# Eight-chunk operand tiles, a bonus by split products, and later joins in a hybrid decoder block

## The chip, the cores and the metric

The kernel runs on one core of one Trainium2 chip. The core has TensorE (PE), whose matrix products write to PSUM, VectorE (DVE), ScalarE (ACT), GpSimd (POOL) and SyncE (SP, which here only issues transfers); each works through its own instructions in order. The metric is the device time in microseconds of one execution, lower is better.

## The reference, cut to what matters

One decoder block on 2048 tokens of width 1024, in float32. The first stage is the one that the change concerns. Half of the mixer is RWKV-7 time mixing with 8 heads of 64:

```python
h = rmsnorm(x, norm_mix[l])
p = h @ w_in[l]
y_ret = retention_mixer(p[..., :RET_PROJ], ...)      # chunks of 128
y_rwkv = rwkv7_mixer(p[..., RET_PROJ:], ...)
...
def step(state, inp):                                # in wkv7_scan, one token after the other
    r_t, w_t, k_t, v_t, a_t, b_t = inp
    sa = jnp.einsum('bhvk,bhk->bhv', state, a_t)
    state = (state * w_t[:, :, None, :] + sa[..., None] * b_t[:, :, None, :]
             + v_t[..., None] * k_t[:, :, None, :])
    return state, jnp.einsum('bhvk,bhk->bhv', state, r_t)
...
bonus = jnp.sum(rh * kh * r_k.astype(jnp.float32), axis=-1, keepdims=True) * vh
return (y + bonus.reshape(B, S, W)) * g
```

Then `x + y @ w_out`, a cross-attention into 256 memory tokens, an MLP with a squared ReLU and a last RMS norm.

## The kernel before, in words

The work has two stages. The first makes the mixer's output and the products of the memory's weights; the second, of two halves of 1024 tokens, does the rest. The change lies in the first.

There the recurrence is computed in chunks of 64 tokens. A **block** is 512 tokens (8 chunks) of one pair of heads, so there are 16 blocks, numbered by `n = 4 * b + pr`; in tile names the two digits are `b` and `pr` (block 5 is `11`, block 8 is `20`). A pair's two heads lie on the two halves of the partitions (`hs[0]`, `hs[1]`). For each block:

- `rwkv_prep` makes the operands: from keys, decays and rates the tiles `BK` and `kk`, then `AR` (the scaled keys and receptances of each chunk, later overwritten in its other half by masked products `psc`), `SR`, `X` (whose other half receives the values, through the products `pvt` and a ScalarE copy, L516) and `BKt` (the transposition `pk` of `BK`). It ends with the bonus: `rS` becomes r times k times r_k, an fp32 product with a matrix of ones sums it over each head (`pb`), and the result is multiplied into the values.
- `diagonal` inverts the 16x16 diagonal pieces of the chunk matrices by small VectorE steps (`Tm`, `Tb`), and `inverses` joins them to inverses of 64x64: VectorE transposes (`TD`, L579), TensorE multiplies (`ph_1`, `ph_2`), VectorE transposes again (`TA`, L593), and TensorE multiplies (`pg_1`, `pg_2`). These four products are called the join below.
- `rwkv_chain` runs the chunks one after the other, each with three hops on TensorE (`ch`) and writes by VectorE, ScalarE and GpSimd between them (`rh`, `X`, `Sd`); the state travels through `X`.

The dense products (`mm..`, `rmq`, `rmv`: projections of the input, in three split products hi x hi, hi x lo, lo x hi each, of operands in fp32r) stand between all of this. The order of TensorE's instructions is fixed by `weave`: eight streams (chains, diagonals, joins, preparations, retention heads, post-processing, transpositions of the input, dense work) are generators. A stream's `yield u` says that its next step is written only after `u` us of TensorE work by the writer's own estimates (`te["us"]`), and meanwhile the other streams, in the order of the list, write theirs. TensorE executes exactly in that order. VectorE's, ScalarE's and GpSimd's orders are set by the framework's scheduler, after priorities and a time line of its own. PSUM has two banks for the small products of this stage (`ps_sc`, tag `sc`), used in turn, so that the second transposition `pk_1` writes the bank out of which `X` is copied.

`split(hi, lo, x, eng)` writes x as a sum of two fp32r tiles: a ScalarE copy (L183) and a subtraction on VectorE or GpSimd (L184).

Of the kernel before, what the change touches and what calls it, by code (L numbers as in the profile page):

```python
# [125 lines left out]
def hybrid_block(tc, a, out, dbg=None, halves=2, stages="012"):  # L126
# [154 lines left out]
    if "1" in stages:  # L281
        with ExitStack() as ctx:
# [65 lines left out]
            def rotary_tables():  # L348
# [18 lines left out]
                AQ.dma_start(out=rot[:, :, 0, :], in_=t3(cc))  # L367
                AQ.dma_start(out=rot[:, :, 1, :], in_=t3(nn))


            Sst = one.tile([P, 4, C], F32, name="Sst")
            V.memset(Sst, 0.0)
# [25 lines left out]
            def rwkv_prep(n, pr, tok0, kS, wa, nm):  # L398
# [82 lines left out]
                AR, SR, X, BKt = ([], []), [], ([], []), []  # L481
                yield lambda: ("R", n) in done and ("C", n - 2, NCH) in done
                rS, vS = done["R", n]
                for g in range(2):
                    for h in range(2):
                        ar = gp.tile([P, 4, P], F32, tag=f"AR{h}", name=f"AR{h}{nm}_{g}", bufs=4)
                        AR[h].append(ar)
                        A.activation(out=ar[hs[h], :, 0:C], in_=ch(kk)[hs[h], g4[g]], func=AF.Copy, scale=-1.0)
                        V.tensor_tensor(out=ar[hs[h], :, C:], in0=ch(rS)[hs[h], g4[g]], in1=Pe[hs[h], g4[g], 1:], op=ALU.mult)
                yield LAT[7]  # L490
                for g in range(2):
                    sr = gp.tile([P, 4, C], F32, tag="SR", name=f"SR{nm}_{g}", bufs=4)
                    SR.append(sr)
                    psc = [ps_sc.tile([P, 4, P], F32, tag="sc", name=f"psc{nm}_{g}{h}") for h in range(2)]
                    for i in range(4):
                        for h in range(2):
                            mm(psc[h][:, i, :], BK[hs[h], 4 * g + i, :, :], AR[h][g][hs[h], i, :], True, True)
                    bc = lambda rows, c0, c1: mk[rows, :, c0:c1].broadcast_to([64, 4, c1 - c0])
                    for h in range(2):
                        q = hs[1 - h]  # L500
                        V.tensor_tensor(out=AR[h][g][q], in0=psc[h][q], in1=bc(q, 0, P), op=ALU.mult)
# [51 lines left out]
            def inverses(n, Mx, TT, nm):  # L553

                a_, b_ = [slice(0, 32), slice(64, 96)], [slice(32, 64), slice(96, 128)]
                TA = gp.tile([P, NCH, 32], F32, tag="TA", name=f"TA{nm}", bufs=1)

                def step(j, rows, op, dst):
                    pg = ps_sc.tile([P, NCH, 32], F32, tag="sc", name=f"pg{nm}_{j}")
                    for c in range(NCH):  # L560
                        for h in range(2):
                            op(pg[rows[h], c, :], c, h)
                    for h in range(2):
                        A.activation(out=dst(h), in_=pg[rows[h]], func=AF.Copy)


                q_ = [slice(32 * q, 32 * q + 32) for q in range(4)]
                own = lambda q: 32 * (q % 2)
                TD = gp.tile([P, NCH, C], F32, tag="TD", name=f"TD{nm}", bufs=1)
                TC = gp.tile([P, NCH, 16], F32, tag="TC", name=f"TC{nm}", bufs=1)  # L570

                def half(j, op, rows=32):
                    pg = ps_sc.tile([P, NCH, 16], F32, tag="sc", name=f"ph{nm}_{j}")
                    for c in range(NCH):
                        for q in range(4):
                            op(pg[32 * q : 32 * q + rows, c, :], c, q)
                    return pg

                tc.keep_in_program_order(V.transpose(TD.rearrange("p c t -> p (c t)"), TT.rearrange("p c t -> p (c t)")))  # L579
                yield 1.5  # L580
                pg = half(1, lambda o, c, q: mm(o, Mx[q_[q], c, own(q) : own(q) + 32], TD[q_[q], c, own(q) : own(q) + 16], True, True))
                A.activation(out=TC, in_=pg, func=AF.Copy)
                yield LAT[6]
                pg = half(2, lambda o, c, q: mm(o, TC[q_[q], c, :], TT[q_[q], c, own(q) + 16 : own(q) + 32], True, True), 16)
                for q in range(4):
                    src = pg[32 * q : 32 * q + 16]
                    dst = TT[32 * q : 32 * q + 16, :, own(q) + 16 : own(q) + 32]
                    if q % 2:
                        V.tensor_copy(out=dst, in_=src)
                    else:  # L590
                        A.activation(out=dst, in_=src, func=AF.Copy)
                for h in range(2):
                    V.transpose(TA[a_[h]], TT[a_[h], :, 0:32])  # L593
                yield 2.0
                step(1, b_, lambda o, c, h: mm(o, Mx[a_[h], c, 32:64], TA[a_[h], c, :], True, True), lambda h: TA[b_[h]])
                yield LAT[6]
                step(2, a_, lambda o, c, h: mm(o, TA[b_[h], c, :], TT[b_[h], c, 32:64], True, True), lambda h: TT[a_[h], :, 32:64])
                done["pg", n] = True

            def rwkv_chain(n, pr, tok0, nm, SR, AR, X, BKt, TT, PC, rn, bon):  # L600

                Y = ps_y.tile([P, NCH, C], F32, tag="y", name=f"Y{nm}")
                for h in range(2):
                    G.tensor_copy(out=X[h][0][hs[h], 0, :], in_=Sst[hs[h], pr, :])
                for c in range(NCH):
                    g, i = divmod(c, 4)
                    chp = ps_ch.tile([P, 512], F32, tag="ch", name=f"ch{nm}_{c}")
                    Sd = gp.tile([P, C], F32, tag="Sd", name=f"Sd{nm}_{c}")
                    rh = gp.tile([P, C], F32, tag="rh", name=f"rh{nm}_{c}")
                    for h in range(2):  # L610
                        mm(chp[hs[h], 0:64], AR[h][g][:, i, 0:C], X[h][g][:, i, :], True, True)
                    with tc.high_priority(URGENT):
                        V.tensor_copy(out=rh, in_=chp[:, 0:64])
                        for h in range(2):
                            G.tensor_scalar(out=Sd[hs[h], :], in0=X[h][g][hs[h], i, :], scalar1=PC[hs[h], c : c + 1],  # L615
                                            scalar2=None, op0=ALU.mult)
                    yield HOP[0]
                    for h in range(2):
                        mm(chp[hs[h], 64:128], TT[hs[h], c, :], rh[hs[h], :], True, True)
                    for h in range(2):  # L620
                        mm(Y[hs[h], c, :], X[h][g][:, i, :], AR[h][g][:, i, C:], True, False)
                    with tc.high_priority(URGENT):
                        A.activation(out=X[0][g][hs[0], i, :], in_=chp[hs[0], 64:128], func=AF.Copy, scale=rn[hs[0], c : c + 1])  # L623
                        V.tensor_scalar(out=X[1][g][hs[1], i, :], in0=chp[hs[1], 64:128], scalar1=rn[hs[1], c : c + 1],
                                        scalar2=None, op0=ALU.mult)
                    yield HOP[1]
                    for h in range(2):
                        mm(chp[hs[h], 128:192], BKt[g][:, i, hs[h]], X[h][g][:, i, :], True, True)
                    for h in range(2):
                        mm(Y[hs[h], c, :], X[h][g][hs[h], i, :], SR[g][hs[h], i, :], False, True)  # L630
                    with tc.high_priority(URGENT):
                        for h in range(2):
                            dst = X[h][(c + 1) // 4][hs[h], (c + 1) % 4, :] if c + 1 < NCH else Sst[hs[h], pr, :]
# [785 lines left out]
```

## Time and profile before

| | |
|---|---|
| median of 3 runs | 3496.29 us (3493.16 to 3503.72) |
| profiled execution | 3505.42 us, span 3503.4 us |
| TensorE products | 3337.0 us busy, 95% of the span, 23328 instructions |
| TensorE weight loads | 2734.7 us, 78% (they overlap the products) |
| VectorE | 2086.9 us, 60%, 3657 instructions |
| ScalarE | 1223.3 us, 35%, 1974 instructions |
| GpSimd | 1619.2 us, 46%, 1325 instructions |
| mean granted TensorE clock | 0.976 |

A share is an average over two stages with different neighbours of TensorE. Matrix products are pipelined, so a row's length is more than the time until the next can start; that time is the distance between the starts of two rows. An fp32 product shows as two records. The granted clock is 1.0 at 2.4 GHz and 0.5 at 1.2 GHz.

### The profile page before, as it was taken

The numbers are of one execution on the slowest core, as the hardware profiler recorded it, in microseconds if no ns is written. First come the engines' busy times: TensorE is split into PE (matmuls) and PEld (weight loads), VectorE is DVE, ScalarE is ACT, GpSimd is POOL, SyncE is SP. The second block draws the span as 40 slices with busy tenths as digits, with TensorE's granted clock in tenths as the row PEclk, the third lists the DMA queues.
The fourth block names the chain that finished last, engine by engine and source line by source line (L and its number), as shares of the span: only waits on it lengthen the run. The fifth ranks groups of instructions, "written<-read, shape, count | busy, mean of one in ns | idle before, by whom it ended". The sixth has DMA issues, their size and how long they took to land.

```text
span 3503.4 us, 57596 instructions
## 1 busy us (share of the span) xinstructions
PE 3337.0 (95%) x23328; PEld 2734.7 (78%) x23328; DVE 2086.9 (60%) x3657; ACT 1223.3 (35%) x1974; POOL 1619.2 (46%) x1325
## 2 busy tenths in 40 slices
PE   7899999999999999989999999999999999999998
PEld 6667777777787777878887888888788878888886
DVE  5755565456645654544775565566648765556557
ACT  4442333233323232434344333333443343333333
POOL 5544323232323232434456555555645465555555
PEclk9999999999999999999999999999999999999999
DMA  7434333333333332473111111111441111111111
GB/s 254 156 131 157 130 98 112 113 130 99 118 113 119 96 113 98 146 282 103 43 49 43 55 55 49 54 54 50 147 142 49 37 49 55 48 55 55 49 55 48
DMA packets 147160, 333.35 MB, mean 95 GB/s; under 512 B 52048, under 2 KB 62800, under 8 KB 146896
## 3 DMA queue, kind: packets, MB, share of 16 engines
q1 hardware_dynamic: 129632, 299.43, 25.7%
q10 hardware_dynamic: 17264, 30.26, 2.4%
q8 instruction: 183, 3.00, 0.4%
q14 instruction: 81, 0.66, 0.1%
HBM read 269.34 MB, written 60.29 MB: 94 GB/s over the span
## 4 chain that ended last, share of the span: by engine, by line
PE 50%; DVE 5%; issue 2%; ACT 1%; POOL 1%; DVEq 0%; POOLq 0%; ACTq 0%
PE up L141 20%; PE o L141 4%; PE tms L141 4%; PE m3d L141 3%; PE m6d L141 3%; PE m4d L141 2%; PE m2d L141 2%; PE m1d L141 2%; PE m5d L141 2%; PE m7d L141 2%; DVE xr L1146 2%; DVE pe L1258 1%; PE pskv L141 1%; PE m3v L141 1%; PE psqk L141 1%
## 5 line engine op out<-in xcount | busy, mean ns | idle before, releaser
L141 PE MATMUL up<-uc,whi 128*128 128x512 f32 x2048 | 633.2, 390 | 5.6 <-ACT uc L1117 5.6
L141 PEld LDWEIGHTS up<-uc,whi 128*128 128x128 f32 x2048 | 384.4, 188 | 86.8 <-ACT uc L1117 6.6
L141 PE MATMUL up<-uc,wlo 128*128 128x512 f32 x1024 | 398.9, 390 | 0.0
L184 POOL TENSOR_TENSOR wlo<-wraw,whi 128x1024 fp32r<-128x1024 f32 x103 | 253.2, 2459 | 281.3 <-ACT whi L183 268.3
L183 ACT ACTIVATE whi<-wraw 128x1024 fp32r<-128x1024 f32 x175 | 184.7, 1058 | 390.5 <-PE up L141 139.5
L615 POOL TENSOR_SCALAR Sd<-X,PC 64x64 f32<-64x64 f32 x256 | 123.9, 484 | 312.3 <-DVE X L634 298.2
L184 DVE TENSOR_TENSOR wlo<-wraw,whi 128x1024 fp32r<-128x1024 f32 x72 | 104.1, 1446 | 255.8 <-ACT whi L183 255.7
L184 POOL TENSOR_TENSOR wlo<-s,whi 128x1024 fp32r<-128x1024 f32 x60 | 159.4, 2658 | 180.5 <-ACT whi L183 180.5
L141 PEld LDWEIGHTS up<-uc,wlo 128*128 128x128 f32 x1024 | 192.3, 188 | 40.1
L141 PE MATMUL tms<-whi,ub 128*128 128x256 f32 x1024 | 192.2, 286 | 0.0
L184 POOL TENSOR_TENSOR wlo<-bd,whi 128x1024 fp32r<-128x1024 f32 x64 | 166.0, 2595 | 51.5 <-ACT whi L183 51.5
L184 POOL TENSOR_TENSOR f<-au,f 128x1024 fp32r<-128x1024 f32 x40 | 112.2, 2804 | 133.6 <-ACT f L183 133.6
L141 PE MATMUL o<-whi,f 128*128 128x512 f32 x512 | 162.6, 398 | 1.4 <-issue 1.4
L141 PEld LDWEIGHTS tms<-whi,ub 128*128 128x128 f32 x1024 | 161.1, 191 | 0.4
L141 PE MATMUL rmq<-whi,hh 128*128 128x256 f32 x512 | 150.5, 294 | 0.0
L141 PE MATMUL rmq<-whi,hl 128*128 128x256 f32 x512 | 149.8, 293 | 0.0
L141 PE MATMUL rmq<-wlo,hh 128*128 128x256 f32 x512 | 149.8, 292 | 0.0
L141 PE MATMUL tms<-wlo,ub 128*128 128x256 f32 x512 | 145.4, 284 | 0.0
L1305 ACT ACTIVATE au<-up 128x512 f32<-128x512 f32 x128 | 75.2, 587 | 194.6 <-PE up L141 194.6
L623 ACT ACTIVATE X<-ch,rn 64x64 f32<-64x64 f32 x128 | 39.3, 307 | 282.5 <-PE Y L141 266.7
L1077 POOL TENSOR_TENSOR s<-bd,bd 128x1024 f32<-128x1024 f32 x48 | 122.2, 2548 | 33.8 <-DMA bd<-w_down 29.4
L183 ACT ACTIVATE whi<-bd 128x1024 fp32r<-128x1024 f32 x64 | 67.6, 1057 | 189.3 <-PE m2d L141 63.6
(1065 smaller groups left out, 9181.5 us busy)
## 6 DMA issues: line engine op xcount, KB each, us to landing
bd<-w_down SPq DMA_DIRECT2D x64, 512.0 KB
wraw<-w_up SPq DMA_DIRECT2D x64, 512.0 KB
whi<-kepthiw SPq DMA_DIRECT2D x45, 512.0 KB
wlo<-keptlow SPq DMA_DIRECT2D x45, 512.0 KB
whi<-kepthim SPq DMA_DIRECT2D x36, 512.0 KB
wlo<-keptlom SPq DMA_DIRECT2D x36, 512.0 KB
wraw<-w_out SPq DMA_DIRECT2D x32, 512.0 KB
xs<-x SPq DMA_DIRECT2D x16, 512.0 KB
```

The costliest lines, as they stand in the source:

```text
L141: pinned(TE.matmul(o, l, r, start=start, stop=stop), us)
L183: A.activation(out=hi, in_=x, func=AF.Copy)
L184: eng.tensor_tensor(out=lo, in0=x, in1=hi.bitcast(F32), op=ALU.subtract)
L615: G.tensor_scalar(out=Sd[hs[h], :], in0=X[h][g][hs[h], i, :], scalar1=PC[hs[h], c : c + 1], scalar2=None, op0=ALU.mult)
L623: A.activation(out=X[0][g][hs[0], i, :], in_=chp[hs[0], 64:128], func=AF.Copy, scale=rn[hs[0], c : c + 1])
L1077: eng.tensor_tensor(out=into, in0=x, in1=y, op=op)
L1146: V.tensor_tensor(out=xv, in0=xv, in1=ps, op=op)
L1258: V.tensor_scalar(out=pe[:, t, :], in0=pe[:, t, :], scalar1=sm[:, t : t + 1], scalar2=None, op0=ALU.mult)
L1305: A.activation(out=r, in_=ps, func=AF.Relu)
```

## The change

`AR` and `X` become one tile of eight chunks for each head instead of two of four (two buffers instead of four, so the same memory), and each is written by one instruction instead of two. The copies into `X` now stand right behind the products `pvt`, and the second head's goes to VectorE. The bonus's `rS` is split in two fp32r tiles, which are multiplied with an fp32r copy of the ones (made once). In `inverses` two yields are doubled.

```diff
+            ones_r = one.tile([P, P], F32R, name="ones_r")
+            A.activation(out=ones_r, in_=c_("ones"), func=AF.Copy)
...
-                for g in range(2):
-                    for h in range(2):
-                        ar = gp.tile([P, 4, P], F32, tag=f"AR{h}", name=f"AR{h}{nm}_{g}", bufs=4)
-                        AR[h].append(ar)
-                        A.activation(out=ar[hs[h], :, 0:C], in_=ch(kk)[hs[h], g4[g]], func=AF.Copy, scale=-1.0)
-                        V.tensor_tensor(out=ar[hs[h], :, C:], in0=ch(rS)[hs[h], g4[g]], in1=Pe[hs[h], g4[g], 1:], op=ALU.mult)
+                for h in range(2):
+                    ar = gp.tile([P, NCH, P], F32, tag=f"AR{h}", name=f"AR{h}{nm}", bufs=2)
+                    AR.append(ar)
+                    A.activation(out=ar[hs[h], :, 0:C], in_=ch(kk)[hs[h]], func=AF.Copy, scale=-1.0)
+                    V.tensor_tensor(out=ar[hs[h], :, C:], in0=ch(rS)[hs[h]], in1=Pe[hs[h], :, 1:], op=ALU.mult)
...
+                for h in range(2):
+                    x = gp.tile([P, NCH, C], F32, tag=f"X{h}", name=f"X{h}{nm}", bufs=2)
+                    if h:
+                        V.tensor_copy(out=x[hs[1 - h]], in_=pv_[hs[1 - h]])
+                    else:
+                        A.activation(out=x[hs[1 - h]], in_=pv_[hs[1 - h]], func=AF.Copy)
+                    X.append(x)
                 yield 0
...
-                    for h in range(2):
-                        x = gp.tile([P, 4, C], F32, tag=f"X{h}", name=f"X{h}{nm}_{g}", bufs=4)
-                        A.activation(out=x[hs[1 - h]], in_=pv_[hs[1 - h], g4[g], :], func=AF.Copy)
-                        X[h].append(x)
                     yield 0.8
...
-                mm(pb, c_("ones"), rS, True, True)
+                rh_ = tp.tile([P, BLK], F32R, tag="E", name=f"rh{nm}b")
+                rl_ = tp.tile([P, BLK], F32R, tag="A", name=f"rl{nm}b")
+                split(rh_, rl_, rS, V)
+                mm(pb, ones_r, rh_, True, False)
+                mm(pb, ones_r, rl_, False, True)
...
-                yield 1.5
+                yield 3.0
                 pg = half(1, lambda o, c, q: mm(o, Mx[q_[q], c, own(q) : own(q) + 32], TD[q_[q], c, own(q) : own(q) + 16], True, True))
...
-                yield 2.0
+                yield 4.0
                 step(1, b_, lambda o, c, h: mm(o, Mx[a_[h], c, 32:64], TA[a_[h], c, :], True, True), lambda h: TA[b_[h]])
```

The remaining lines of the diff only follow the tiles' new indices (`X[h][:, c, :]` for `X[h][g][:, i, :]`).

TensorE's order before, in the join of block 5, from its second product to its third (`rsR` are products of a retention head, `pss` and the `mm12` rows belong to the preparation of the next block):

```order
L141 MATMUL ph_2_5729<-TT_162,TC_5635 16x16 x32
L141 MATMUL ch_4_5625<-X_10_1_4788,BKt_1_4801 64x64
...
L141 MATMUL Y_5239<-SR_1_4645,X_10_1_4790 64x64
L141 MATMUL rsR_5774<-qkTR_5676 128x128
...
L141 MATMUL rsR_5775<-qkTR_5725 128x128
L141 MATMUL pg_1_5788<-TA_5633,Mx_4984 32x32 x16
L141 MATMUL ch_5_5807<-X_10_1_4788,AR_10_1_4550 64x64
```

And the same place now:

```order
L141 MATMUL ph_2_5692<-TT_164,TC_5575 16x16 x32
L141 MATMUL ch_4_5601<-X_10_4712,BKt_1_4749 64x64
...
L148 MATMUL pqR_5737<-cs,rq_5504 128x128 x4
L141 MATMUL mm12r<-hl,whi_5560 128x512
L141 MATMUL mm12r<-hh,wlo_5561 128x512
...
L141 MATMUL rsR_5749<-qkTR_5688 128x128
...
L141 MATMUL ch_5_5763<-X_10_4712,AR_10_4503 64x64
L141 MATMUL ch_5_5763<-X_10_4714,AR_10_4506 64x64
L141 MATMUL pss_5771<-cs,sq_5628 64x1 x16
L141 MATMUL pg_1_5791<-TA_5573,Mx_4921 32x32 x16
```

A transposition and five dense products have moved ahead of the third product, and so have the next chunk's first chain product and `pss`, which followed it.

ScalarE's order before, at the copies into `X` of block 8 (`rb` is the last step of the post-processing of an earlier block that ScalarE has there):

```order
L388 ACTIVATE ts21r<-mm21r,pv 128x512
L659 ACTIVATE rb_8721<-st_13_8718 128x512
L516 ACTIVATE X_20_0_8754<-pvt_8732 64x256
L516 ACTIVATE X_20_0_8756<-pvt_8732 64x256
L516 ACTIVATE X_20_1_8769<-pvt_8732 64x256
L516 ACTIVATE X_20_1_8771<-pvt_8732 64x256
L520 ACTIVATE BKt_0_8762<-pk_0_8749 128x512
```

And now, on the same engine:

```order
L391 ACTIVATE ts21r<-mm21r,pv 128x512
L668 ACTIVATE rb_8613<-st_13_8610 128x512
L516 ACTIVATE X_20_8706<-pvt_8689 64x512
L525 ACTIVATE BKt_0_8719<-pk_0_8710 128x512
L525 ACTIVATE BKt_1_8730<-pk_1_8721 128x512
```

One copy of twice the width stands where four stood, behind the same `rb`. The other head's copy is in VectorE's order, between steps of the next block's diagonal inversion:

```order
L550 TENSOR_TENSOR Tb_8491<-Tb_8491,Tm_8615 128x8x9
L546 TENSOR_TENSOR Tm_8615<-Lb_8489,Tb_8491 128x8x8
L514 COPY X_20_8708<-pvt_8689 64x512
L550 TENSOR_TENSOR Tb_8491<-Tb_8491,Tm_8615 128x8x8
L546 TENSOR_TENSOR Tm_8615<-Lb_8489,Tb_8491 128x8x7
```

Before, no row of VectorE stood there for `X`.

## Rows read from the trace of the kernel before

**Rows 1.** Stretches: their length, then busy us (instructions) by engine, clock, DMA.

```profile
0.00:1480.00 1480.00, 1371.74 (x13844) 1096.94 (x13845) 849.53 (x2134) 474.72 (x943) 528.62 (x824) 0.96 0.39 128
1480.00:3503.00 2023.00, 1965.21 (x9486) 1637.73 (x9484) 1237.35 (x1524) 748.53 (x1032) 1090.57 (x502) 0.99 0.21 71
```

**Rows 2.** TensorE's waits, 0 to 1480 us: us in total, times, longest.

```profile
PE pg L141 <- DVE TA L593: 15.9, 9, 4.6
PE pk L148 <- ACT X L516: 13.4, 8, 3.8
PE ch L141 <- DVE X L624: 13.4, 16, 2.8
...
PE ch L141 <- DVE X L634: 5.6, 8, 1.4
...
PE ph L141 <- DVE TD L579: 3.9, 4, 1.3
```

**Rows 3.** TensorE's time line at block 1's bonus: start, us, instruction.

```profile
149.94 0.39 PE L141 MATMUL mm02r<-hh,wlo 128*128 128x512 f32 x1
150.17 1.02 PE L141 MATMUL pb<-rS01r,cs 128*128 128x512 f32 x2
151.12 0.34 PE L141 MATMUL ch<-X,AR 128*64 128x64 f32 x4
```

**Rows 4.** Instructions by tile or line, ns min/median/max; the last row: busy, mean ns.

```profile
L516 ACT ACTIVATE X<-pvt x64: 358/378/382, 95.2 to 1346.5; 64x256 f32<-64x256 f32 x64
L520 ACT ACTIVATE BKt<-pk x32: 577/597/600, 96.6 to 1351.9; 128x512 f32<-128x512 f32 x32
L184 DVE TENSOR_TENSOR wa<-wf,wa 128x512 fp32r<-128x512 f32 x3 | 2.1, 686 | 0.5 <-ACT wa L183 0.5
```

**Rows 5.** Time line at block 8's copies into X.

```profile
787.37 0.63 ACT L659 ACTIVATE rb<-st 128x512 f32<-128x512 f32 x1 [7.07 <-POOL st L681]
...
788.01 1.55 ACT L516 ACTIVATE X<-pvt 64x256 f32<-64x256 f32 x4
...
789.61 0.66 PE L148 MATMUL pk<-cs,BK 128*128 128x128 f32 x4 [3.83 <-ACT X L516]
```

**Rows 6.** Time line of block 5's join; in brackets the idle time before.

```profile
505.22 1.16 PE L141 MATMUL rsR<-qkTR 64*128 64x128 f32 x16
...
509.58 0.60 DVE L634 SCALAR_TENSOR_TENSOR X<-ch,PC,Sd 64x64 f32<-64x64 f32 x2
...
511.01 0.31 PE L141 MATMUL pg<-TA,Mx 32*32 32x32 f32 x2 [4.63 <-DVE TA L593]
...
512.60 0.44 DVE L593 STREAM_TRANSPOSE TA<-TT 32x256 f32<-32x256 f32 x1
513.09 1.06 PE L141 MATMUL pg<-TA,Mx 32*32 32x32 f32 x30 [1.77 <-DVE TA L593]
```

**Rows 7.** TensorE's time line in block 13's join.

```profile
1210.96 0.31 PE L141 MATMUL pg<-TA,Mx 32*32 32x32 f32 x2 [4.63 <-DVE TA L593]
1211.74 1.05 PE L141 MATMUL pg<-TA,Mx 32*32 32x32 f32 x30 [0.47 <-DVE TA L593]
```

**Rows 8.** Five short stretches at clock 0.50, the first and the sum.

```profile
575.72:579.13 3.41, 3.15 (x10) 1.88 (x8) 3.25 (x8) 2.73 (x5) 2.52 (x3) 0.50 0.00 0
...
sum 20.47, PE 20.21 PEld 14.33 DVE 10.90 ACT 7.07 POOL 6.76; mean PE 4.04 PEld 2.87 DVE 2.18 ACT 1.41 POOL 1.35
```

**Rows 9.** Four long stretches at clock 0.50, that of block 5 and the sum.

```profile
507.45:521.11 13.66, 8.33 (x121) 6.96 (x122) 6.00 (x13) 2.60 (x7) 3.80 (x5) 0.50 0.00 1
...
sum 54.61, PE 42.69 PEld 31.54 DVE 21.36 ACT 14.60 POOL 16.42; mean PE 10.67 PEld 7.88 DVE 5.34 ACT 3.65 POOL 4.11
```

**Rows 10.** Time line of VectorE's diagonal steps beside GpSimd.

```profile
93.35 4.68 POOL L184 TENSOR_TENSOR wlo<-wraw,whi 128x1024 fp32r<-128x1024 f32 x2 [6.96 <-ACT whi L183]
...
95.90 2.23 DVE L537 TENSOR_TENSOR Tm<-Lb,Tb 128x72 f32<-128x72 f32 x1
...
98.16 0.23 DVE L541 TENSOR_TENSOR Tb<-Tb,Tm 128x72 f32<-128x72 f32 x1
```

More of the change, by code (lines that the diff above doesn't have):

```diff
@@ L479, in rwkv_prep @@
                 done["L", n] = Lb, Tb, Mx, TT_[gi % 2], Ts, nm
-                AR, SR, X, BKt = ([], []), [], ([], []), []
+                AR, SR, X, BKt = [], [], [], []
                 yield lambda: ("R", n) in done and ("C", n - 2, NCH) in done
                 rS, vS = done["R", n]
-                for g in range(2):
-                    for h in range(2):
-                        ar = gp.tile([P, 4, P], F32, tag=f"AR{h}", name=f"AR{h}{nm}_{g}", bufs=4)
-                        AR[h].append(ar)
-                        A.activation(out=ar[hs[h], :, 0:C], in_=ch(kk)[hs[h], g4[g]], func=AF.Copy, scale=-1.0)
-                        V.tensor_tensor(out=ar[hs[h], :, C:], in0=ch(rS)[hs[h], g4[g]], in1=Pe[hs[h], g4[g], 1:], op=ALU.mult)
+                for h in range(2):
[3 more added lines that the diff above has]
+                    V.tensor_tensor(out=ar[hs[h], :, C:], in0=ch(rS)[hs[h]], in1=Pe[hs[h], :, 1:], op=ALU.mult)
                 yield LAT[7]
@@ L496, in rwkv_prep @@
                         for h in range(2):
-                            mm(psc[h][:, i, :], BK[hs[h], 4 * g + i, :, :], AR[h][g][hs[h], i, :], True, True)
+                            mm(psc[h][:, i, :], BK[hs[h], 4 * g + i, :, :], AR[h][hs[h], 4 * g + i, :], True, True)
                     bc = lambda rows, c0, c1: mk[rows, :, c0:c1].broadcast_to([64, 4, c1 - c0])
@@ L500, in rwkv_prep @@
                         q = hs[1 - h]
-                        V.tensor_tensor(out=AR[h][g][q], in0=psc[h][q], in1=bc(q, 0, P), op=ALU.mult)
+                        V.tensor_tensor(out=AR[h][q, g4[g]], in0=psc[h][q], in1=bc(q, 0, P), op=ALU.mult)
                         V.tensor_tensor(out=sr[hs[h]], in0=psc[h][hs[h], :, C:], in1=bc(hs[h], C, P), op=ALU.mult)
@@ L603, in rwkv_chain @@
                 for h in range(2):
-                    G.tensor_copy(out=X[h][0][hs[h], 0, :], in_=Sst[hs[h], pr, :])
+                    G.tensor_copy(out=X[h][hs[h], 0, :], in_=Sst[hs[h], pr, :])
                 for c in range(NCH):
@@ L610, in rwkv_chain @@
                     for h in range(2):
-                        mm(chp[hs[h], 0:64], AR[h][g][:, i, 0:C], X[h][g][:, i, :], True, True)
+                        mm(chp[hs[h], 0:64], AR[h][:, c, 0:C], X[h][:, c, :], True, True)
                     with tc.high_priority(URGENT):
@@ L614, in rwkv_chain @@
                         for h in range(2):
-                            G.tensor_scalar(out=Sd[hs[h], :], in0=X[h][g][hs[h], i, :], scalar1=PC[hs[h], c : c + 1],
+                            G.tensor_scalar(out=Sd[hs[h], :], in0=X[h][hs[h], c, :], scalar1=PC[hs[h], c : c + 1],
                                             scalar2=None, op0=ALU.mult)
@@ L620, in rwkv_chain @@
                     for h in range(2):
-                        mm(Y[hs[h], c, :], X[h][g][:, i, :], AR[h][g][:, i, C:], True, False)
+                        mm(Y[hs[h], c, :], X[h][:, c, :], AR[h][:, c, C:], True, False)
                     with tc.high_priority(URGENT):
-                        A.activation(out=X[0][g][hs[0], i, :], in_=chp[hs[0], 64:128], func=AF.Copy, scale=rn[hs[0], c : c + 1])
-                        V.tensor_scalar(out=X[1][g][hs[1], i, :], in0=chp[hs[1], 64:128], scalar1=rn[hs[1], c : c + 1],
+                        A.activation(out=X[0][hs[0], c, :], in_=chp[hs[0], 64:128], func=AF.Copy, scale=rn[hs[0], c : c + 1])
+                        V.tensor_scalar(out=X[1][hs[1], c, :], in0=chp[hs[1], 64:128], scalar1=rn[hs[1], c : c + 1],
                                         scalar2=None, op0=ALU.mult)
@@ L627, in rwkv_chain @@
                     for h in range(2):
-                        mm(chp[hs[h], 128:192], BKt[g][:, i, hs[h]], X[h][g][:, i, :], True, True)
+                        mm(chp[hs[h], 128:192], BKt[g][:, i, hs[h]], X[h][:, c, :], True, True)
                     for h in range(2):
-                        mm(Y[hs[h], c, :], X[h][g][hs[h], i, :], SR[g][hs[h], i, :], False, True)
+                        mm(Y[hs[h], c, :], X[h][hs[h], c, :], SR[g][hs[h], i, :], False, True)
                     with tc.high_priority(URGENT):
                         for h in range(2):
-                            dst = X[h][(c + 1) // 4][hs[h], (c + 1) % 4, :] if c + 1 < NCH else Sst[hs[h], pr, :]
+                            dst = X[h][hs[h], c + 1, :] if c + 1 < NCH else Sst[hs[h], pr, :]
                             V.scalar_tensor_tensor(out=dst, in0=chp[hs[h], 128:192], scalar=PC[hs[h], c : c + 1],
```

## The prediction

> **What bounds the kernel now.** I read the page first: TensorE is busy for 95% of the span, VectorE for 60%, so a change shows only where it alters what TensorE does or waits for. Every edit lies in the first stage, up to about 1480 us, and the table by stretches splits the span there [rows 1]: TensorE is idle for 108 us of those 1480 and its mean granted clock is 0.96, against 58 us idle and 0.99 in the other 2023. Those 108 us, and the time that the clock stands at 1.2 GHz, are the most that a better order can win; the work itself is the rest. TensorE's list of waits in that stage names what ends them [rows 2]. The largest entry is the join's first product (pg) behind VectorE's transposition TA, 15.9 us in nine waits. The second is the transposition pk behind ScalarE's copies of X, 13.4 us in eight. The chain's products (ch) behind VectorE's writes of X cost 13.4 + 5.6 us, and the join's earlier product (ph) behind the transposition TD costs 3.9 us with none above 1.3. The change touches all five.
>
> The sums below are waits and work of the profiled execution, which took 3505.4 us (span 3503.4 and 2.0 around it), 9.1 above the median of the runs, 3496.3. I subtract the sum from the median. About 0.3%, 10.5 us, is what a measurement of this kernel can tell from no change.
>
> **The bonus product.** The timeline shows the fp32 product pb starting at 150.17 and the next product at 151.12, so it holds TensorE for 0.95 us [rows 3]. A split (fp32r) product of the same 128x512 shape is the row ahead of it, 149.94 to 150.17, 0.23 us. Two of them take 0.46, so each of the 16 blocks saves 0.49 us: **-7.8 us**, and this is work, not a wait. If the weight load of the second product were not covered it would be less; as the row of 0.23 us is one of a stream with changed weights, I keep the value, with -4 as the poorer bound (half of it). The price is one more ScalarE copy and one more VectorE subtraction of 128x512 in each block, 0.60 us by BKt's copy of that size and 0.69 by the split of wa [rows 4]. By the order both stand many instructions ahead of pb, before the block's products of AR, so TensorE doesn't wait for them: cost nothing while that lead holds, and 16 x 1.29 = 21 us if it were gone. The buffers that they take (of kk and Pi) are free by then, and the next block's first writes of them come behind pb's place in TensorE's order anyway.
>
> **The eight-chunk tiles.** AR's writes become half as many and twice as long. Nothing in rows 2 waits for them, so I give that nothing; a first product that needs the whole tile comes some 0.3 us later than behind a half. For X, four ScalarE copies of 0.378 us (1.51) [rows 4] become one of twice the width, about 0.60 by BKt's row, and one on VectorE, about 0.69 by wa's. pk's second transposition writes the bank that the copies read, so it waits for the last. Block 8 shows it: ScalarE finishes rb, then copies X from 788.01 for 1.55 us, and pk starts at 789.61 after 3.83 us of idle [rows 5]. The order leaves rb ahead of X, so the wait shrinks by 0.91 us and doesn't go. Eight waits at 0.91 are 7.3 at best; several are shorter than 0.91 and VectorE's half can be the later one. I take **-5 us**.
>
> **The joins.** Each step is written 1.5 us (ph) and 2.0 us (pg) of TensorE work later than it was. ph's waits are all below 1.5, so 3.9 us go. For pg, two blocks hold most of it. In block 5 TensorE ends its products rsR at 506.4, waits 4.63 us, issues two and waits 1.77 more, until the second TA ends at 513.04 [rows 6]; VectorE is late there because it works off a queue, not because the transposition is long (0.44 us). In block 13 it is 4.63 and 0.47 [rows 7]. The order shows that what is moved ahead of pg in block 5 is five dense products and chunk 5's first chain product, and the latter reads the X that VectorE ends at 510.18, so part of the wait moves to it; each of these two blocks gives 2.0 us and keeps the rest. The other five waits, 15.9 - 6.4 - 5.1 = 4.4 us, go. Sum: 3.9 + 2.0 + 2.0 + 4.4 = **-12.3 us**. Bounds: 0, if what VectorE does ahead of TA moves along with the join, and -19.8, if all of both entries goes.
>
> **The clock.** At 1.2 GHz stand, among others, five short stretches that follow such waits, 20.5 us with TensorE busy for 20.2 [rows 8], and four of 13.65 us that lie on joins, busy for 42.7 [rows 9]. In the second list TensorE waited in front of, or inside, each. Work at 1.2 GHz takes twice its time at 2.4, so if all of them went, (20.2 + 42.7) / 2 = 31 us would come back. The two long ones of blocks 5 and 13 hold the waits that stay, and waits elsewhere can let the clock fall anew. I take a quarter, **-8 us**, between 0 and -31.
>
> **What the new order costs.** Every chain product meets other neighbours, and VectorE gets 16 x (0.69 + 0.69) = 22 us more work, 2.6% of the 850 us that it is busy in the stage. The chain waits of 13.4 + 5.6 us are the ones that answer to a fuller VectorE queue. By its share they would grow by half a microsecond; were they to grow by all of themselves, by 19. I take **+6 us**, nearer to the first.
>
> Sum: -7.8 - 5 - 12.3 - 8 + 6 = -27 us, and 3496 - 27 is **3469 us**. No load is added, and SP's queue carries the same transfers. A later join delays nothing at the stage's end, since in TensorE's order the memory's last dense products still stand behind the chain's last step.
>
> **Rivals.**
>
> *The clock comes back* (0.12). If joins spread among dense products keep the clock at 2.4 GHz in all nine stretches, the term is -31 and the sum -50: 3446. For it speaks that the long stretch of block 5 holds only 8.3 us of work in 13.66, a gap which the change fills up; against it that the queue in front of TA stays.
>
> *The waits only move* (0.18). VectorE works in order, so a product moved behind TA may meet another late result of the same queue. Then terms two to five cancel and only the product of the bonus remains, with ±6 for a reshuffled order: 3488, within 0.3%. For it speaks block 5, where chunk 5's product takes over part of the wait.
>
> *VectorE's half of X is late* (0.10), the slower case. The copy stands behind whatever VectorE does at that moment, in block 8 between the steps of the diagonal's inversion. One of these, 128x72, took 2.23 us at 95.90 while GpSimd ran its subtractions from 93.35; its neighbour of the same size took 0.23 [rows 10]. Behind the copy in VectorE's queue stand further steps of that inversion and the chain's copies rh, which would be late with it. If pk waits 2.2 us longer in all 16 blocks, that is 35 us, and 16 falls of the clock of 3.4 us (the length of the short stretches in rows 8) with 1.7 us lost in each add 27: 3469 + 5 for the gain not made + 62 = 3536. From 1.7 us a block on (27/16) the waits alone cancel the sum. In two blocks of three it gives 3469 + 5 + 41 = 3515, and that many have to be so unlucky for the kernel to be slower by more than can be told. The Trainium skill (SBUF — State Buffer, "Who interferes with whom") says that a VectorE instruction with two SBUF inputs and a GpSimd instruction that reads SBUF lock each other out for a whole instruction. By that rule the new subtraction of the bonus is exposed as well, and with one such GpSimd subtraction (4.68 us for two) ahead of each it would put 16 x 2.34 = 37 us more into VectorE's queue; the slow row above agrees with the rule.
>
> **How the numbers follow.** The forecast itself, a gain of 11 to 45 us, has 0.60. With the clock's rival 0.72 is faster by over 0.3%; 0.18 is within; 0.10 slower. The range goes from 3440, just past the clock's rival, to 3500, past the rival in which the waits only move; above it lies the slower case, below it a few chances in a hundred.
>
> **What would show it.** pb as two rows 0.23 us apart; the entry pk behind X near 8 us, with releasers L516 or the new VectorE copy; ph behind TD gone; pg behind TA at 6 to 8 us, nearly all in blocks 5 and 13; a mean clock in the first stage of 0.97; the stage's end some 27 us earlier. The prediction is wrong if TensorE's idle time in the stage stays near 108 us (then the waits moved: look at ch and at whatever follows the join), if pk waits for VectorE's copy, or if the second stage, which the change doesn't touch, differs by more than 3 us.

## The result and the profile after

The changed kernel takes 3481.66 us (median of 6 runs, 3476.54 to 3485.54), the kernel before, in 6 runs beside it, 3503.19 us. The ratio is **0.9936 [0.9919, 0.9954]**: 0.64% faster, some 22 us. That is inside the range and on the forecast side, 5 us short of the predicted gain of 27. (In time it is 13 us above 3469: the kernel before itself came out 7 us slower in these runs than in the three that the prediction started from.) The profiled executions took 3505.42 us before (span 3503.4) and 3478.59 after (span 3476.4).

First the table by stretches. The first stage ends where the memory's last dense product ends, at 1549.5 us before and 1522.9 after. Before:

```profile
0.00:1549.50 1549.50, 1432.12 (x14208) 1150.11 (x14208) 889.54 (x2183) 502.30 (x975) 557.73 (x836) 0.96 0.40 135
1549.50:3503.40 1953.90, 1904.84 (x9121) 1584.56 (x9120) 1197.34 (x1475) 720.95 (x999) 1061.46 (x489) 0.99 0.19 64
```

After, with the row that answers to the first of [rows 1] ahead of them:

```profile
0.00:1480.00 1480.00, 1386.78 (x14016) 1117.58 (x14016) 876.92 (x2155) 473.35 (x892) 542.96 (x829) 0.96 0.40 132
0.00:1522.90 1522.90, 1423.14 (x14208) 1148.01 (x14208) 903.34 (x2183) 491.28 (x912) 562.69 (x836) 0.96 0.41 137
1522.90:3476.40 1953.50, 1904.71 (x9121) 1584.27 (x9120) 1197.58 (x1475) 720.76 (x999) 1061.53 (x489) 0.99 0.19 64
```

The whole gain lies in the first stage (26.6 us); the second differs by 0.4. TensorE's idle time in the stage falls from 117.4 us to 99.8, and its busy time from 1432.1 to 1423.1. VectorE is busy for 13.8 us more. Up to 1480 us, where the prediction set its mark, TensorE is idle for 93.2 us instead of 108.3.

TensorE's waits up to 1480 us (us in total, times, longest), to be read against [rows 2]:

```profile
PE ch L141 <- DVE X L633: 21.8, 11, 4.3
...
PE ch L141 <- DVE rh L622: 6.9, 8, 2.6
...
PE ch L141 <- DVE X L643: 4.7, 5, 1.5
PE pg L141 <- ACT TA L573: 4.5, 1, 4.5
PE rYR L141 <- DVE sTR L772: 3.8, 2, 1.9
PE pk L148 <- ACT BKt L525: 3.7, 3, 2.4
PE pg L141 <- DVE X L514: 3.0, 1, 3.0
...
PE pb L141 <- DVE X L514: 0.8, 1, 0.8
...
PE pg L141 <- DVE TA L602: 0.4, 1, 0.4
PE pk L148 <- DVE X L514: 0.4, 1, 0.4
```

The joins' entry has all but gone (pg behind VectorE's TA: 15.9 to 0.4), ph behind TD isn't there any more, and pk's 13.4 have become 4.1. The chain's products pay for part of it: behind X they wait 21.8 + 4.7 us where it was 13.4 + 5.6, and one pg now waits for ScalarE.

Block 1's bonus on TensorE's time line, as [rows 3]: the next product starts 0.45 us after pb's first, where it was 0.95.

```profile
143.64 0.39 PE L141 MATMUL pb<-rh_01b,ones_r 128*128 128x512 f32 x1
143.86 0.39 PE L141 MATMUL pb<-rl_01b,ones_r 128*128 128x512 f32 x1
144.09 0.40 PE L141 MATMUL mm02r<-hh,whi 128*128 128x512 f32 x1
```

Block 8's copies into X, as [rows 5]. The two halves take 0.59 and 0.68 us. The weight load of pk's second set waits 0.23 us, and that for ScalarE's BKt; its product, which waited 3.83 us, waits for nothing:

```profile
776.70 0.63 ACT L668 ACTIVATE rb<-st 128x512 f32<-128x512 f32 x1 [1.01 <-POOL st L690]
...
779.01 0.59 ACT L516 ACTIVATE X<-pvt 64x512 f32<-64x512 f32 x1 [1.67 <-PE pvt L141]
779.66 0.68 DVE L514 COPY X<-pvt 64x512 f32<-64x512 f32 x1
780.28 0.42 PEld L148 LDWEIGHTS pk<-cs,BK 128*128 128x128 f32 x4 [0.23 <-ACT BKt L525]
780.32 0.62 PE L148 MATMUL pk<-cs,BK 128*128 128x128 f32 x4
```

Block 5's join on the same view, as [rows 6]. The pg that waited 4.63 and 1.77 us comes at 516.87 and waits for nothing. The chain product behind ph (chunk 4's) waits 2.35 us for X. It stood at that place before too, and waited 0.34 us: VectorE wrote its X at 504.35 then, ahead of the first product for BK, and writes it now behind that product. Chunk 5's first product, which the prediction saw waiting, comes without a wait:

```profile
510.36 0.29 DVE L633 TENSOR_SCALAR X<-ch,rn 64x64 f32<-64x64 f32 x1
510.71 0.42 PE L141 MATMUL ch<-X,BKt 128*64 128x64 f32 x4 [2.35 <-DVE X L633]
...
515.58 0.34 PE L141 MATMUL ch<-X,AR 128*64 128x64 f32 x4
...
516.87 0.69 PE L141 MATMUL pg<-TA,Mx 32*32 32x32 f32 x32
```

On that join the clock now stands at 1.2 GHz for 3.4 us (from 510.8) instead of 13.66 [rows 9]. Three longer stretches remain or are new, the last of them on block 13's join, where it is longer than it was. No wait of a join stands at their beginnings; each begins at, or within a microsecond of, a wait of a retention head's product behind VectorE's sTR (2.47, 1.93 and 1.92 us, the last of them shown):

```profile
637.10:647.30 10.20, 9.85 (x199) 7.17 (x198) 4.48 (x11) 2.51 (x7) 2.15 (x3) 0.50 0.13 43
852.20:862.40 10.20, 9.85 (x103) 7.68 (x105) 4.44 (x12) 2.19 (x5) 1.92 (x3) 0.50 0.00 0
1190.10:1210.60 20.50, 19.75 (x164) 15.26 (x164) 6.96 (x18) 4.45 (x10) 4.40 (x8) 0.50 0.13 34
...
1190.85 0.47 PE L141 MATMUL rYR<-sTR,rv 128*64 128x128 f32 x1 [1.92 <-DVE sTR L772]
```

### The profile page after: what moved, and what is told of

It reads as the page before. It is cut to its first block, busy times and chain, and to the rows that moved or that the text cites. A ratio compares the mean times of both kernels' runs of the same rounds, so it can differ in the third digit from the quotient of the medians.

```text
span 3476.4 us, 57568 instructions
## 1 busy us (share of the span) xinstructions
PE 3327.9 (96%) x23328; PEld 2732.3 (79%) x23328; DVE 2100.9 (60%) x3657; ACT 1212.0 (35%) x1911; POOL 1624.2 (47%) x1325
## 3 DMA queue, kind: packets, MB, share of 16 engines
q1 hardware_dynamic: 129632, 299.43, 25.7%
## 4 chain that ended last, share of the span: by engine, by line
PE 50%; DVE 5%; POOL 1%; issue 1%; ACT 1%; DMA 0%; DVEq 0%; ACTq 0%; POOLq 0%
PE up L141 20%; PE o L141 4%; PE tms L141 4%; PE m3d L141 3%; PE m6d L141 3%; PE m4d L141 2%; PE m2d L141 2%; PE m1d L141 2%; PE m5d L141 2%; PE m7d L141 2%; DVE xr L1155 1%; DVE pe L1267 1%; PE pskv L141 1%; PE m3v L141 1%; PE psqk L141 1%
## 5 line engine op out<-in xcount | busy, mean ns | idle before, releaser
L1155 DVE TENSOR_TENSOR xr<-xr,m3d 128x512 f32<-128x512 f32 x128 | 80.0, 681 | 88.8 <-PE m3d L141 86.2
```

What stands on the lines that cost most here:

```text
L1155: V.tensor_tensor(out=xv, in0=xv, in1=ps, op=op)
```

## The experiments

The change has three parts: P, the bonus by fp32r products; T, the tiles of eight chunks with the copies of X; and Y, the two numbers behind which the joins are written. The first kernels run every combination of the three, then come the dose of Y and what hides in P. Ratios are against the kernel before, run beside each, with their intervals.

One table serves them all. Every run lists its span and mean granted clock. Span x clock is about what the span would be with TensorE at 2.4 GHz throughout, so it shows work and waits; span x (1 - clock) is what the clock takes (a little less in truth, since waits at 1.2 GHz lose nothing). Both are means over a kernel's runs; the standard error of the last column is 1 to 3 us, of the one before it 0.4 to 2. The experiments were run in three groups, each on another chip; the kernel before differs between the groups by 1.1 us at most in work and waits and by 2.7 in the clock.

```
kernel                           ratio  [interval]         runs  clock   span x clock  span x (1-clock)
before                           1                           70  0.9777     3420.8         77.9
after            P T Y           0.9936 [0.9919, 0.9954]      6  0.9793     3406.9         71.9
e1_product       P               1.0019 [1.0004, 1.0034]     11  0.9748     3418.7         88.3
e2_yields            Y           0.9939 [0.992,  0.9958]      5  0.9802     3410.4         68.9
e3_tiles           T             1.0001 [0.9985, 1.0018]     12  0.9776     3421.3         78.5
e4_no_yields     P T             1.0021 [1.0005, 1.0037]     12  0.9733     3414.5         93.6
e5_no_product      T Y           0.99   [0.9886, 0.9914]      4  0.9828     3403.4         59.7
e12_yields_product P Y           0.9972 [0.9958, 0.9986]     12  0.9788     3412.5         74.1
e7_half_yields   half of Y       0.9971 [0.9957, 0.9985]     12  0.9791     3415.7         73.0
e8_more_yields   Y and half more 0.994  [0.9926, 0.9955]      6  0.9827     3417.3         60.3
e9_product_order P, old order    1.0033 [1.002,  1.0047]      6  0.9743     3420.5         90.1
e11_split_unused split alone     1.0015 [0.9998, 1.0031]     12  0.9765     3422.7         82.4
e10_placebo      order alone     1.0047 [1.0031, 1.0063]      7  0.9730     3419.6         94.9
e13_hop          T Y, HOP        0.9904 [0.9883, 0.9925]      5  0.9830     3405.5         58.9
```

**The product alone** (P: the diff's lines on ones_r, rh_, rl_ and pb).

> The kernel before with the bonus by two fp32r products alone. Terms add up: TensorE has 7.8 us less work, ratio 0.9978, pb falls from 0.95 to 0.46 us a block, and the waits pg behind TA (15.9 us) and pk behind X (13.4 us) stay within 3 us. Rival, the redrawn order decides: as the bonus's virtual time is shorter, later steps stand elsewhere, and the time differs from 0.9978 by more than 6 us either way, with other waits than before.

It is slower, by 0.19%. pb is two products as expected, so the work is saved; but TensorE's waits up to 1485 us show the chain's products behind X at 25.7 us, against 13.4 in [rows 2]:

```profile
PE ch L141 <- DVE X L631: 25.7, 20, 4.7
...
PE pg L141 <- DVE TA L600: 7.5, 8, 2.5
```

and over its runs the clock takes 88.3 us where it took 77.9. The waits of pg behind TA fell from 15.9 to 7.5 though nothing was done to the joins: the waits are others than before, as the rival said.

**The later joins alone** (Y).

```diff
-                yield 1.5
+                yield 3.0
...
-                yield 2.0
+                yield 4.0
```

> The kernel before with the two doubled yields alone. Terms add up: -12.3 us of waits in the joins, -8 of clock, +6 in the chain, ratio 0.9960; pg behind TA below 7 us, ph behind TD none. Rival, the waits only move: TA and TD's waits go, but the chain's (ch behind X and rh, 23.2 us before) grow by as much, the stage's idle time stays within 4 us of 117, ratio 0.999 to 1.001.

Nearly the whole gain of the change: 0.9939. Its waits up to 1480 us, with pk behind the old copies of X still there (pg behind TA is down to 1.0 us, ph behind TD to 1.8):

```profile
PE ch L141 <- DVE X L624: 12.8, 11, 3.0
...
PE pk L148 <- ACT X L516: 9.3, 5, 5.0
```

**The tiles alone** (T: the lines on AR and X).

> The kernel before with the eight-chunk tiles and the earlier, divided copy of X alone. Terms add up: -5 us, ratio 0.9986, pk behind X from 13.4 to about 8. Rival, VectorE's half is late: pk waits for the copy on VectorE, more than 13 us in total, ratio above 1.001. Rival, ScalarE's queue was the whole cause: pk's waits fall below 3 us, ratio 0.997.

No change, 1.0001. The wait of pk isn't gone: it has gone to the copy BKt, which stands behind X on ScalarE, and to VectorE's half.

```profile
PE pg L141 <- DVE TA L595: 15.5, 8, 4.6
...
PE ch L141 <- DVE X L626: 11.5, 13, 3.4
PE pk L148 <- ACT BKt L522: 9.3, 4, 4.3
...
PE pk L148 <- DVE X L511: 3.6, 5, 1.5
```

**The change without the later joins** (P and T; in the changed kernel the two numbers go back to 1.5 and 2.0).

> The changed kernel with the two yields put back to 1.5 and 2.0. Terms add up: -13 us against before, ratio 0.9963, waits of the joins as before. If the joins are nearly all of the gain: 0.999 to 1.000. If the joins gave nothing because their waits moved into the chain: 0.9936, as the whole change.

1.0021, above all that was expected: without Y the rest of the change is a small loss. The chain's products wait twice as long behind X as in e3:

```profile
PE ch L141 <- DVE X L633: 23.1, 19, 3.7
```

**The change without the product** (T and Y; in the changed kernel).

```diff
-            ones_r = one.tile([P, P], F32R, name="ones_r")
-            A.activation(out=ones_r, in_=c_("ones"), func=AF.Copy)
...
-                rh_ = tp.tile([P, BLK], F32R, tag="E", name=f"rh{nm}b")
-                rl_ = tp.tile([P, BLK], F32R, tag="A", name=f"rl{nm}b")
-                split(rh_, rl_, rS, V)
-                mm(pb, ones_r, rh_, True, False)
-                mm(pb, ones_r, rl_, False, True)
+                mm(pb, c_("ones"), rS, True, True)
```

> The changed kernel with the bonus as one fp32 product again. If the product is worth its 7.8 us in the changed order: ratio 0.9958 against 0.9936 of the whole. If it is taken back as in the run with the product alone (1.0019, where the chain's waits grew from 23 to 36 us): 0.992 to 0.994, no worse than the whole.

**0.9900**, 3464.65 us: faster than both kernels, and by 0.36% faster than the change itself. The clock takes 59.7 us in its runs, 12.2 less than in those of the changed kernel. Of the waits up to 1480 us the chain's behind X are smaller by half than after (behind rh they are larger, 11.3 us against 6.9):

```profile
PE ch L141 <- DVE rh L615: 11.3, 10, 3.8
PE ch L141 <- DVE X L626: 6.9, 7, 1.8
PE ch L141 <- DVE X L636: 6.4, 4, 2.6
```

**The later joins with the product** (Y and P, the old tiles).

> The kernel before with the doubled yields and the product, without the eight-chunk tiles. If the product costs 0.2 to 0.4% whatever stands beside it: 0.996 to 0.998. If terms are lost in the redrawing and only the whole is what it is: anything from 0.990 to 1.000.

0.9972, so 0.33% behind e2: the fourth pair in which the product costs. The chain's products wait for 24.7 us behind X, against 12.8 in e2:

```profile
PE ch L141 <- DVE X L631: 24.7, 13, 3.7
```

**The dose of Y**, on the kernel before: half of it (2.25 and 3.0), and half as much again:

```diff
-                yield 1.5
+                yield 4.5
...
-                yield 2.0
+                yield 6.0
```

> The kernel before with yields of 2.25 and 3.0, between those of before and the doubled ones. If the yields' gain is the wait they take away: a part of it, ratio 0.996 to 0.998, pg and ph together at 6 to 15 us. If the doubled yields' 0.9939 was a lucky redrawing: no order among the three, ratio above 1.000.

> The kernel before with yields of 4.5 and 6.0. The doubled yields left 2.8 us of waits at pg. If the yields work by taking the joins' waits away, there is nothing left to take and the ratio stays at 0.993 to 0.995, with pg and ph together below 6 us and the clock's time at 1.2 GHz near 102 us. If instead every redrawing moves the time by several us, it lands outside, by more than 5 us either way.

1, 0.9971, 0.9939, 0.9940 for Y at 0, half, whole and one and a half. The gain grows with the dose and is full at the change's own numbers. In e8 the clock still gains (60.3 us) while work and waits lose (3417.3 against 3410.4). The times came as expected, the waits in the profiles did not: in e7 ph waits for 15.3 us behind TD, 12.2 of them at once, and in e8 pg waits for 13.7 us behind SR and the chain's products for 37.8 behind X and rh.

**The product in the old order.** The order is made by a count of TensorE's work, so a cheaper pb moves everything behind it. One line more in e1 counts pb as before, and TensorE's order is then that of the kernel before.

```diff
                 mm(pb, ones_r, rh_, True, False)
                 mm(pb, ones_r, rl_, False, True)
+                te["us"] += 2 * 512 / 2400
```

> The product alone, but written with the fp32 product's virtual time, so that TensorE's order is that of before except for pb itself. If the redrawn order took the product's gain back: chain's waits at 23 us as before and ratio 0.9978. If the split's own work on VectorE and ScalarE did it (18 us more of VectorE): chain's waits above 30 us and ratio 1.000 to 1.002.

1.0033, no better than e1 and above what was expected, so a redrawn order on TensorE isn't needed for the loss (the orders of VectorE and ScalarE did change a little with the added instructions). Work and waits are those of before (3420.5) although 8 us of work are saved, and the clock takes 12.2 us more. Up to 1480 us the chain's products wait for 24.7 us behind X and rh, about as before (23.2); it is the joins that wait longer, 21.9 us behind TA where it was 15.9:

```profile
PE pg L141 <- DVE TA L601: 21.9, 13, 4.6
```

In its profile three stretches at 1.2 GHz are long, where before had none or one of 3.4 us, and TensorE is busy all through them:

```profile
455.70:465.90 10.20, 10.06 (x66) 7.33 (x65) 3.05 (x6) 1.33 (x4) 0.10 (x1) 0.50 0.36 112
578.50:595.60 17.10, 17.10 (x123) 12.10 (x118) 4.05 (x11) 3.22 (x8) 5.78 (x10) 0.50 0.18 63
1271.40:1295.30 23.90, 23.81 (x225) 17.11 (x226) 10.25 (x29) 6.69 (x15) 9.32 (x13) 0.50 0.15 45
```

The first two begin where pg has just waited for TA. In the kernel before it came without a wait in the first of these joins, and waited 0.80 us in the second:

```profile
454.80 0.69 PE L141 MATMUL pg<-TA,Mx 32*32 32x32 f32 x30 [1.19 <-DVE TA L601]
...
578.00 0.71 PE L141 MATMUL pg<-TA,Mx 32*32 32x32 f32 x30 [1.65 <-DVE TA L601]
```

The third has no such wait ahead of it. The 10 us before it, and at the same place of the kernel before the 10 us ahead and the 24 that follow:

```profile
1261.40:1271.40 10.00, 8.85 (x121) 5.76 (x118) 4.44 (x11) 5.59 (x14) 2.13 (x3) 1.00 0.45 152
```

```profile
1262.00:1272.00 10.00, 9.25 (x123) 5.92 (x121) 4.65 (x11) 5.26 (x13) 2.13 (x3) 1.00 0.43 149
1272.00:1296.00 24.00, 21.89 (x288) 16.14 (x287) 12.26 (x34) 7.50 (x17) 10.13 (x16) 0.93 0.25 90
```

TensorE did 0.4 us less in those 10 us, with two short waits (0.53 and 0.61 us) in the last three of them, and then stood at 1.2 GHz for 23.9 us; in the kernel before it fell for one short stretch.

**The split without its products.** The split is computed and not used, and pb stays one fp32 product; nothing of the reference's work is left out.

```diff
+                rh_ = tp.tile([P, BLK], F32R, tag="E", name=f"rh{nm}b")
+                rl_ = tp.tile([P, BLK], F32R, tag="A", name=f"rl{nm}b")
+                split(rh_, rl_, rS, V)
                 mm(pb, c_("ones"), rS, True, True)
```

> The kernel before with the split of the bonus's operand computed on ScalarE and VectorE and not used: the product stays fp32, TensorE's order stays. It leaves nothing out. If the split's work on VectorE and ScalarE takes the product's gain back: ratio 1.003 to 1.006 (the 1.0033 of the product in the old order, without its 9 us of saved work), waits at ch, pg and pk together above 60 us. If the load is harmless and the shorter product itself did it (TensorE less busy beside the joins, its clock at 1.2 GHz for 160 instead of 137 us): ratio 0.999 to 1.001 and 137 us.

1.0015 [0.9998, 1.0031]: the load of the split may be half of the loss, but the interval reaches to nothing, and so does the difference of the clock (4.5 us with an error of 2.8). The waits say more. TensorE's order is that of before here too, no product has changed, and pg waits behind TA as in e9:

```profile
PE pg L141 <- DVE TA L596: 22.3, 14, 4.6
```

**An order redrawn for no reason**, by a twentieth more in one latency of the plan.

```diff
-LAT = (6.0, 5.0, 2.0, 13.0, 10.0, 3.0, 1.0, 4.0, 8.0, 8.0, 12.0)
+LAT = (6.0, 5.0, 2.0, 13.0, 10.0, 3.0, 1.0, 4.0, 8.4, 8.0, 12.0)
```

> The kernel before with one delay of the retention heads at 8.4 instead of 8.0 us: no instruction more or less, TensorE's order redrawn in some 1900 places. It measures what a redrawing alone does. If little: ratio 0.999 to 1.001 and the waits at pg, pk and ch within 4 us of 17, 15 and 23. If much: several us either way, which would be the measure for any single term of that size.

1.0047, a larger step than P or T made alone. All of it is clock: it takes 17.0 us more, work and waits 1.2 less. One of the long stretches of its profile, again with TensorE busy throughout, begins behind a wait of a join:

```profile
1292.08 0.69 PE L141 MATMUL pg<-TA,Mx 32*32 32x32 f32 x30 [2.21 <-DVE TA L593]
...
1292.70:1309.80 17.10, 17.10 (x120) 12.14 (x117) 4.79 (x12) 3.22 (x8) 2.55 (x7) 0.50 0.11 33
```

**Chain steps written later**, on e5, since ch is the largest wait left.

```diff
-HOP = (1.8, 1.8, 1.8)
+HOP = (2.1, 2.1, 1.8)
```

> Tiles and yields without the product (0.9900), and the chain's first two hops written 2.1 instead of 1.8 us of TensorE work apart. What is left of the joins' lesson: the chain's waits (26.7 us) shrink where 0.3 us more work stands ahead of each of 256 hops. Same mechanism: ch below 18 us and ratio 0.987 to 0.989. Rival, the chain becomes too long and the stage's end waits for it, or the redrawing costs it: above 0.990.

0.9904, the time of e5 and not the 0.987 to 0.989 that were expected. The profile's waits of ch fell from 26.7 us (2.2 of them behind Sst) to 17.2, and those at pk and ph rose by 6.8.

## Why the prediction held, and which step failed

The direction, the size and the range were right, but two terms were wrong in opposite senses, so that the sum is right in part by luck: the product came out 17.7 us worse than forecast and the later joins 12.1 better. With all eight combinations of P, T and Y run, each part's worth is the mean of four differences (with it less without it, the others equal), in work and waits and in clock:

```
part   work and waits   clock    sum     predicted
P          -0.8         +10.7    +9.9     -7.8
T          -4.1          -1.4    -5.5     -5
Y         -10.5         -15.9   -26.4     -14.3 (joins -12.3, clock -8, new order +6)
```

The sum of the parts is -22.0 us; after less before is -19.9 by the same table. The clock's -8 and the new order's +6 were forecast for the change as a whole; they stand beside Y, since the first was tied to the waits of the joins, but the second was priced from work that P and T put on VectorE.

**The bonus product is the step that failed**: "each of the 16 blocks saves 0.49 us: -7.8 us, and this is work, not a wait". The saving at pb is real (0.50 us a block by the rows of block 1), but the time doesn't come back. In the four pairs work and waits change by -2.1, -6.8, +2.1 and +3.5 us (e1 less before, e4 less e3, e12 less e2, after less e5), so other waits take nearly all of it, and the clock takes 10.4, 15.1, 5.2 and 12.2 more. So P costs some 0.2 to 0.4% in every pair.

Where the saved work went can be read from the profiles, of one execution each. In each of the four pairs the chain's products wait 12 to 15 us longer behind X with P than without (25.7 against 13.4, 23.1 against 11.5, 24.7 against 12.8, 21.8 against 6.9). In e9, with TensorE's old order, they don't (14.6), and pg waits 6 us longer behind TA; e11 has those 6 us too, without the products. So in the old order it is the split on the other engines (with the small changes that it makes in their orders) that goes with the joins' longer waits, and two of e9's three long stretches at 1.2 GHz begin at such waits. How much of the clock's 10.7 us comes that way stays open: the third stretch begins without one, the times of e11 can't be told from those of before, and none of the four differences is clearly larger than the step that e10 made for no reason. What speaks for P is that all four have one sign, and e9's as well.

"Cost nothing while that lead holds" did hold for TensorE: nothing waits for rh_ or rl_. It was VectorE's queue that I priced apart, in the term of the order, at half a microsecond by its share; in e9 and e11 it is 6 us at the joins. The rival's second half, that the new subtraction is locked out by GpSimd in every block (37 us), did not come about: two of the 16 took 1.7 and 1.8 us, the other 14 0.7. One of the two ran beside GpSimd's subtractions from 117.79 (5.14 us for two). It agrees with what the Trainium skill (SBUF — State Buffer, "Who interferes with whom") says of a VectorE instruction with two SBUF inputs beside a GpSimd instruction that reads SBUF:

```profile
L184 DVE TENSOR_TENSOR rl_01b<-rS01r,rh_01b 128x512 fp32r<-128x512 f32 x1 | 1.7, 1718 | 0.0
```

**The tiles** have -5.5 us in the mean where -5 was predicted, but that is luck: the four differences are +1.1, +1.0, -16.1 and -7.8 us. Without Y they gave nothing (1.0001), and the wait only went over to BKt. The copies take 0.592 and 0.682 us in the median, as priced from [rows 4] (0.60 and 0.69). In block 8 the wait went further than "shrinks by 0.91", because rb came earlier: ScalarE sat idle for 1.67 us until X's products were done. The foretold 8 us of pk behind X are 0.4 behind VectorE's copy and 3.7 behind BKt; with 3.0 of pg and 0.8 of pb behind that copy, 13.4 - 7.9 = 5.5 us were saved on that list; in e3's, hardly any (9.3 + 3.6 remain). The slower rival, VectorE's half late in every block, has only those waits of 3.0, 0.8 and 0.4 us.

**The joins** gained more than priced, and in another way. Of pg's 15.9 us behind TA all but 0.4 went, where 6 to 8 were to stay in blocks 5 and 13, and ph's 3.9 behind TD went as foretold: 19.4 us. But ch's waits grew from 23.2 to 33.4 (X and rh, up to 1480 us), and 4.5 of pg behind ScalarE and 3.8 of rYR are new: 18.5 us. On the list of waits alone the rival in which they only move would be right, and block 5 shows one case: a chain product takes over 2.35 of pg's 6.40 us, at its old place in TensorE's order, since VectorE now writes its X later. Yet with Y alone the stage's idle time fell by 17.3 us (117.4 before, 1523.3 - 1423.2 = 100.1 in e2's profile), and over the four pairs work and waits are 10.5 us less; the larger part of Y's worth, 15.9 us, is clock.

**The clock** was put at -8 us in sum, and after less before is -6.0. But that is -15.9 for Y and +10.7 for P: Y's clock is worth twice what I gave the term, and the sum came right because P spent the rest. That falls go with the joins' waits is shown where a stretch begins at such a wait (in e9 and e10) and on block 5's join, where both shrank; it isn't shown for the sum. The three longest stretches that are left begin at other waits, and e10 moved the clock by 17.0 us with no change to the joins' yields. The stage's mean clock in the profile is 0.96, not 0.97; e5's is 0.97.

**The new order** at +6 had no run that isolates it, and e10 shows that it can't be priced at a few microseconds either way: a redrawn order with the same work moved the kernel by 0.47%, in the one case that was tried. The effect of Y stands out from that by its dose (half, whole, one and a half) and by four pairs of one sign (-19 to -37 us); that of T alone does not, and that of P only by its sign.

## What to carry to other kernels

In a kernel that one engine bounds, take from the runs' clocks how much time work and waits take and how much the clock takes, before and after every part of a change: here an edit that saves eight microseconds of matrix work loses nearly all of them to waits elsewhere and ten more by the clock, and the profile's wait list shows only the first. Where instructions are placed by a count of work, run a placebo, the same work in a neighbouring order, before believing any term smaller than its effect (0.47% here), and doses for those larger. And run the parts of a change one by one: the best kernel was the change without one of its three parts (0.9900 [0.9886, 0.9914]).

## What was not expected of the hardware

TensorE can stand at 1.2 GHz for 17 to 24 us with hardly an idle moment, as the profile counts it (23.81 of 23.90 us busy in e9, 17.10 of 17.10 in e10). I had read the long stretches as joins that hold waits, and several do begin at one: 1.19 and 1.65 us in e9, 2.21 in e10. But e9's of 23.90 us came after 10 us in which TensorE was busy for 8.85 and waited for no more than 0.61 us at a time. The Trainium skill (TensorE: Matmul & The Clock Gate, "A second HAM failure mode: psum-queue depth-cycling") tells of a kernel whose clock swings because TensorE is idle for moments between groups of products. The two short waits ahead of that fall agree with it; no run here shows that they are its cause.

One VectorE row, the mixing step of 1024 columns, took 3.44 us where its median is 1.28, beside a GpSimd subtraction; the chain's X stood behind it, and TensorE waited 3.75 us for that:

```profile
189.55 3.44 DVE L307 SCALAR_TENSOR_TENSOR xs<-xs,msa,gmix 128x1024 f32<-128x1024 f32 x1 [0.24 <-POOL msa L179]
189.56 2.35 POOL L184 TENSOR_TENSOR wlo<-wraw,whi 128x1024 fp32r<-128x1024 f32 x1
...
193.50 0.48 PE L141 MATMUL ch<-X,BKt 128*64 128x64 f32 x4 [3.75 <-DVE X L633]
```

It is one of the longest waits of the chain that the change left. The kernel before has one such row too, of 3.40 us.
